# Attention's scores and values in 64x64 quarters of the PE array, and later places for splits, squares, a scaling and a row norm

## The chip, the cores and the metric

The kernel runs on one core of a Trainium2 chip. The metric is the device time of one execution, in microseconds (us). Engines are named as in the profile: PE (TensorE: matrix products and transposes), DVE (VectorE), ACT (ScalarE), POOL (GpSimd) and SP, which issues most DMAs. Each engine works through its own queue in order and they wait for one another by semaphores.

## What is computed

One layer of a streaming encoder over 320 tokens (256 of a new stream, 64 of a running one), width 2048, all in float32:

```python
z = rmsnorm(x, ln_g) @ w_in                       # 2048 -> q 1024, k 128, v 128, zs 2048
# group A: 16 query heads of 64 on 2 key/value heads, chunks of 64 tokens,
# each chunk sees itself and the 2 chunks before it (up to 192 keys)
s = einsum('...qhgd,...khd->...hgqk', q, k) * HEAD_DIM**-0.5 + bias
m = maximum(max(s, -1), sink); p = exp(s - m)
w = p / (sum(p, -1) + exp(sink - m))
attn_o = einsum('...hgqk,...khd->...qhgd', w, v)
# group B: gating, over chunks of 128 tokens
a = gelu(zs); u = a[..., :1024]; v = rmsnorm(a[..., 1024:], g)
sgu_o = u * (einsum('gij,bnjgc->bnigc', ws, v) + b_s)
# both groups
mix = concat([rmsnorm(attn_o, g_a), rmsnorm(sgu_o, g_s)])
x = x + mix @ w_out
h = rmsnorm(x, ln_ffn); y = x + square(relu(h @ w_up)) @ w_down      # 2048 -> 8192 -> 2048
```

Keys, values and the normalised gating rows of the running stream are outputs too.

## The kernel before

**Weights.** Everything is kept transposed: channels on the 128 partitions, the 320 tokens along the free axis. Each weight matrix is streamed from HBM in tiles of 512 x 256 (`w_raw`, 512 KB). A tile is split in two (`halves`): ACT writes the rounded part `w_hi` (L115), DVE the rest `w_lo` (L116), three buffers of each. The activations are split in the same way (`XH`/`XL`, `AH`/`AL`, `SH`/`SL`, ...). A product of a tile is then 24 PE instructions, three for each of 4 x 2 blocks of 128x128: high by high, high by low, low by high (L141). This document calls the work of one tile a step; `product` makes four steps for 256 output columns of `w_in`.

**Small work between the steps.** Attention and gating run during the projection by `w_in`. A function given in `between_pieces` under the number of a step is issued on PE right behind this step's last product, and the next step's products right behind the piece: `tc.issue_after` fixes this order, and `narrow` holds the last PE instruction of the piece. On the other engines the framework's planner sets the order of instructions, from the program's order, the dependencies and a simulated time line; `issue_after` only says what an instruction may not go ahead of on its engine.

**Attention** has ten units: 2 key/value heads (`kv`) x 5 chunks of queries. `attend(i)` is one piece and works on three units at once: it issues the scores of unit i, the transposes of unit i-2 and the values of unit i-3. Scores (L428) are products over the 64 channels of a head for two heads at a time, so they hold 64 rows by 128 columns of the PE array; `p` picks the upper or lower 64 rows, and each `p` writes its own PSUM bank `s_ps[p]` (one buffer each). Softmax runs on DVE (L438 to L448, L455, L456), ACT (L449, L453) and POOL (the division, L457). Transposes (L477) bring the probabilities into `misc` banks (two buffers), DVE copies them to `pts` (L500), and one `attend` later the values (L484, L489) multiply them by the values' rows: `va` for the first two 64-key parts, 128 rows by 64 columns, and `vb` for the third, 64x64. The result stands in columns 384 to 511 of the `misc` banks, and ACT copies it to `ao` (L495). Chunk 0 of a key/value head has 64 keys and only `vb`; chunk 1 has 128 keys and only `va`; chunks 2, 3 and 4 have 192 keys and both.

The pieces stand behind steps 1 and 3 of a product: `attend(0)` and `(1)` in q's last product, `attend(2)` to `(9)` in gating's four products for v, `attend(10)` to `(12)` in the first two products for u.

**Gating.** For v, `gelu2` gives `gv`; squares are summed on POOL into `acc_v` (`add_square`, L512), POOL scales `gv` and `gvs` by a gain (L539) and copies the last 64 sums (L540). `rows_norm` turns the sums into one factor per token: three small PE products (L166), DVE (L169) and a power on POOL (L171). `by_rows` transposes `gv` on PE (L551), and ACT writes it back with that factor (L553); its last call also issues two stores on POOL's queue. `spatial` (L564, L567) multiplies by the gating matrices.

**Behind attention**, in the loop over u's four products (L597), `split` makes `AH` (ACT, L205) and `AL` (DVE, L206) from `ao`, and `add_square` sums its squares into `acc_a`; `two_parts` and `rstd` turn that into the norm `rm_a`, a piece of the fourth product. `AH` and `AL` are first used by the product with `w_out`, and after it come the two large products with `w_up` and `w_down`.

Of the kernel before, what the change touches and what calls it, by code (L numbers as in the profile page):

```python
# [11 lines left out]
AF = mybir.ActivationFunctionType  # L12
# [3 lines left out]
P = 128  # L16
# [10 lines left out]
HD = 64  # L27
# [3 lines left out]
def hymba_step_kernel(ctx: ExitStack, tc: tile.TileContext, i, o):  # L31
# [378 lines left out]
    units = [(b, kv) for kv in range(2) for b in range(5)]  # L410
    probs = {}
    room = blk("vnat", [P, 2432])
# [5 lines left out]

    def scores(u):
        blk_, kv = units[u]  # L420
        q0, k0, nk, b0 = blocks[blk_][0:4]
        js = slice(2 * kv, 2 * kv + 2)
        s_ps = [score_bank(p) for p in range(2)]
        for j in range(2):
            a = 2 * (2 * kv + j)
            for p in range(2):
                hs = slice(p * HD, (p + 1) * HD)
                mm = nc.tensor.matmul(out=s_ps[p][:, j * nk:(j + 1) * nk],  # L428
                                      lhsT=qT[hs, blk_, a:a + 2].rearrange("p a t -> p (a t)"),
                                      rhs=kz[hs, kv, k0:k0 + nk], start=True, stop=True)  # L430
        last = mm
        s = at.tile([P, 2, 2, 192], F32, name="s", tag="s", bufs=2)
# [18 lines left out]
        for p in range(2):  # L451
            for j in range(2):
# [3 lines left out]
        nc.vector.reciprocal(out=den, in_=den)  # L456
        nc.gpsimd.tensor_tensor(out=sv, in0=sv,  # L457
                                in1=den[:, :, :, None].to_broadcast([P, 2, 2, nk]), op=ALU.mult)
        probs[u] = s
        return last  # L460

    def attend(i):

        t, v = i - 2, i - 3
        t, v = t if 0 <= t < 10 else None, v if 0 <= v < 10 else None
        if t is not None or v is not None:
            bank = [misc(), misc()] if t is not None else [score_bank(p) for p in range(2)]

# [4 lines left out]
        if t is not None:  # L473
            s = probs.pop(t).rearrange("x p j k -> x p (j k)")
            nk = blocks[units[t][0]][2]
            cols = ((P, 2),) if nk == HD else ((0, 0), (192, 1)) if nk == P else ((0, 0), (256, 1), (P, 2))
            behind([lambda p=p, x=x, c=c: nc.tensor.transpose(out=bank[p][:, x * P:(x + 1) * P], in_=s[:, p, c:c + P],  # L477
                                                              identity=ident) for p in range(2) for c, x in cols])
        if v is not None:
            blk_, kv = units[v]  # L480
            q0, va, vb = (blocks[blk_][x] for x in (0, 4, 5))
            out = lambda p, j: bank[j][p * HD:(p + 1) * HD, 384:512]
            if va is not None:
                behind([lambda p=p, j=j: nc.tensor.matmul(out=out(p, j), lhsT=va[j][:, kv],  # L484
                                                          rhs=pts[v % 2][p][:, j * P:(j + 1) * P], start=True,
                                                          stop=vb is None) for j in range(2) for p in range(2)])
            if vb is not None:
                hs = [slice(j * HD, (j + 1) * HD) for j in range(2)]
                behind([lambda p=p, j=j: nc.tensor.matmul(out=out(p, j), lhsT=vb[j][hs[j], kv], rhs=pts[v % 2][p][hs[j], 256:384],  # L489
                                                          start=va is None, stop=True) for p in range(2) for j in range(2)])  # L490
        if i < 10:
            behind([lambda: scores(i)])
        if v is not None:
            for j in range(2):
                nc.scalar.activation(out=ao[:, 4 * kv + 2 * j:4 * kv + 2 * j + 2, q0:q0 + 64],  # L495
                                     in_=bank[j][:, 384:512].rearrange("p (a q) -> p a q", a=2), func=AF.Copy)
        if t is not None:
# [33 lines left out]
    for g in range(4):  # L531
# [4 lines left out]
        for a in range(2 * g, 2 * g + 2):  # L536
            add_square(acc_v, gv[:, a], a == 0)
            for dst, c in ((gv[:, a, 0:256], slice(0, 256)), (gvs[:, a], slice(256, T))):
                nc.gpsimd.tensor_scalar(out=dst, in0=gv[:, a, c], scalar1=g_sv[:, a:a + 1], scalar2=None, op0=ALU.mult)  # L539
    nc.gpsimd.tensor_copy(out=acc_v[:, T:TP], in_=acc_v[:, 256:T])  # L540
# [36 lines left out]
    def rows_norm():  # L577
# [4 lines left out]
    u_pieces = {  # L582
        0: {1: lambda: attend(10), 3: lambda: (rows_norm(), attend(11))},
        1: {1: lambda: (attend(12), by_rows((0, 0), (1, 0))), 2: lambda: by_rows((0, 1), (1, 1), (2, 0)),
            3: lambda: spatial(0, 1, 2, 3)},
# [11 lines left out]
    for g in range(4):  # L597
        u_ps = product(w_in, 0, KT, 1280 + g * 256, xh, xl, between_pieces=u_pieces.get(g, {}))
        if g == 0:
            acc_a = sums("acc_a")  # L600
            AH, AL = blk("AH", [P, 8, T], F32R), blk("AL", [P, 8, T], F32R)
        for x in range(2):
            a, (high, low, _) = 2 * g + x, steps[2 * x + 1]
            with tc.issue_after(high), tc.issue_after(low):
                split(ao[:, a], g_oa[:, a:a + 1], AH[:, a], AL[:, a])
        for x, a in enumerate(range(3 * g, min(3 * g + 3, 8))):
            with tc.issue_after(steps[x][0]):
                add_square(acc_a, ao[:, a], a == 0)
# [131 lines left out]
```

## Time and profile before

| | |
|---|---|
| median of 3 runs | 1243.49 us (1242.76 to 1245.67) |
| the profiled execution's own time | 1243.31 us |
| its span, first to last instruction | 1241.5 us |
| PE busy | 1236.9 us, 8524 products and transposes |
| DVE busy | 658.6 us |
| ACT busy | 492.0 us |
| POOL busy | 108.3 us |
| granted PE clock | 1.00 of full speed |
| the products by `w_in` with all pieces (time line) | about 34.8 to 223.9 us |

PE's rows in the profile are modelled at their ends: instructions overlap in the array, and a row lasts longer than the distance to the next one. So the starts of successive rows are what is compared here. A float32 score or value product shows as two rows (two passes), a transpose as one.

### The profile page before, as it was taken

What the parts mean: (1) busy time and instruction counts of PE and PEld (TensorE: products, weight loads), DVE (VectorE), ACT (ScalarE), POOL (GpSimd) and SP (SyncE); (2) the same over time, 40 slices, a digit from 0 to 9 for tenths busy, and PEclk for the clock granted to TensorE, in tenths of its full rate; (3) what the DMA queues carried; (4) which work ended last, traced back from release to release, by engine and by line L of the source; (5) the groups of instructions that cost most, each with busy time, mean ns of one, the idle gap of its engine ahead of it and who ended that gap; (6) DMA issues with size and microseconds to landing.
All of it is one profiled execution on the core that took longest, in us unless ns stands there. A gap on an engine that the chain in (4) does not pass through costs nothing.

```text
span 1241.5 us, 20270 instructions
## 1 busy us (share of the span) xinstructions
PE 1236.9 (100%) x8524; PEld 1226.1 (99%) x8524; DVE 658.6 (53%) x781; ACT 492.0 (40%) x652; POOL 108.3 (9%) x109
## 2 busy tenths in 40 slices
PE   9999999999999999999999999999999999999998
PEld 8999999999999999999999999999999999999998
DVE  7877767977864443444444444444443344544343
ACT  7436555434533333223443233333333323433321
POOL 0137563201300000000000000000000000000000
PEclk9999999999999999999999999999999999999999
DMA  9753445444455444445544444545444444544550
GB/s 278 228 147 106 119 118 176 157 152 145 148 152 152 153 152 147 146 149 153 153 151 145 147 152 153 152 144 149 151 153 153 147 147 149 152 153 164 167 164 32
DMA packets 187995, 188.02 MB, mean 151 GB/s; under 512 B 7648, under 2 KB 187440, under 8 KB 187904
## 3 DMA queue, kind: packets, MB, share of 16 engines
q1 hardware_dynamic: 186640, 185.51, 48.0%
q0 software_dynamic: 832, 0.98, 0.4%
q8 instruction: 66, 1.08, 0.4%
q10 hardware_dynamic: 432, 0.24, 0.1%
q14 instruction: 25, 0.20, 0.0%
HBM read 183.13 MB, written 3.35 MB: 150 GB/s over the span
## 4 chain that ended last, share of the span: by engine, by line
PE 97%; POOL 1%; DMA 1%; DVE 0%; issue 0%; ACT 0%; SPq 0%; DVEq 0%; ACTq 0%; POOLq 0%
PE acc L141 92%; PE misc L141 1%; PE q_ps L237 1%; PE acc L237 1%; PE s_ps L428 1%; DMA w_first<-in_w_in 0%; PE misc L477 0%; DMA xT<-in_xT 0%; POOL acc_a L512 0%; PE misc L484 0%; PE misc L489 0%; PE misc L551 0%; PE g_ps L564 0%; PE misc L564 0%; ACT s L453 0%
## 5 line engine op out<-in xcount | busy, mean ns | idle before, releaser
L116 DVE TENSOR_TENSOR w_lo<-w_raw,w_hi 128x1024 fp32r<-128x1024 f32 x332 | 413.9, 1247 | 429.7 <-ACT w_hi L115 420.9
L115 ACT ACTIVATE w_hi<-w_raw 128x1024 fp32r<-128x1024 f32 x332 | 352.1, 1060 | 689.1 <-PE acc L141 662.7
L141 PE MATMUL acc<-H2H,w_lo 128*128 128x320 f32 x1024 | 316.4, 309 | 0.0
L141 PE MATMUL acc<-H2H,w_hi 128*128 128x320 f32 x1024 | 316.4, 309 | 0.0
L141 PE MATMUL acc<-H2L,w_hi 128*128 128x320 f32 x1024 | 316.4, 309 | 0.0
L141 PE MATMUL acc<-FH,w_hi 128*128 128x320 f32 x992 | 306.5, 309 | 0.0
L141 PE MATMUL acc<-FL,w_hi 128*128 128x320 f32 x992 | 306.5, 309 | 0.0
L141 PE MATMUL acc<-FH,w_lo 128*128 128x320 f32 x992 | 306.5, 309 | 0.0
L141 PEld LDWEIGHTS acc<-H2H,w_hi 128*128 128x128 f32 x1024 | 192.2, 188 | 0.0
L141 PEld LDWEIGHTS acc<-H2L,w_hi 128*128 128x128 f32 x1024 | 192.2, 188 | 0.0
L141 PEld LDWEIGHTS acc<-H2H,w_lo 128*128 128x128 f32 x1024 | 192.2, 188 | 0.0
L141 PEld LDWEIGHTS acc<-FH,w_hi 128*128 128x128 f32 x992 | 186.2, 188 | 0.0
L141 PEld LDWEIGHTS acc<-FL,w_hi 128*128 128x128 f32 x992 | 186.2, 188 | 0.0
L141 PEld LDWEIGHTS acc<-FH,w_lo 128*128 128x128 f32 x992 | 186.2, 188 | 0.0
L141 PE MATMUL acc<-XH,w_hi 128*128 128x320 f32 x352 | 110.7, 314 | 0.0
L141 PE MATMUL acc<-XH,w_lo 128*128 128x320 f32 x352 | 108.8, 309 | 0.0
L141 PE MATMUL acc<-XL,w_hi 128*128 128x320 f32 x352 | 108.7, 309 | 0.0
L141 PEld LDWEIGHTS acc<-XH,w_hi 128*128 128x128 f32 x352 | 66.1, 188 | 3.1 <-issue 2.5
L141 PEld LDWEIGHTS acc<-XL,w_hi 128*128 128x128 f32 x352 | 66.1, 188 | 0.0
L141 PEld LDWEIGHTS acc<-XH,w_lo 128*128 128x128 f32 x352 | 66.1, 188 | 0.0
L656 DVE SCALAR_TENSOR_TENSOR tf<-acc,r 128x640 f32<-128x640 f32 x32 | 26.4, 825 | 41.8 <-PE acc L141 41.8
L671 DVE TENSOR_TENSOR xT<-xT,acc 128x640 f32<-128x640 f32 x31 | 25.5, 821 | 41.8 <-PE acc L141 41.8
(227 smaller groups left out, 1062.9 us busy)
## 6 DMA issues: line engine op xcount, KB each, us to landing
w_raw<-in_w_up SPq DMA_DIRECT2D x128, 512.0 KB
w_raw<-in_w_down SPq DMA_DIRECT2D x128, 512.0 KB
w_raw<-in_w_in SPq DMA_DIRECT2D x44, 512.0 KB
w_raw<-in_w_out SPq DMA_DIRECT2D x32, 512.0 KB
w_first<-in_w_in SPq DMA_DIRECT2D x14, 256.0 KB
out_yT<-xT SPq DMA_DIRECT2D x7, 320.0 KB
xT<-in_xT SPq DMA_DIRECT2D x8, 160.0 KB
xT<-in_xT SPq DMA_DIRECT2D x4, 320.0 KB
```

The source lines that it names most:

```text
L115: return (pin(nc.scalar.activation(out=hi, in_=raw, func=AF.Copy)).ins, pin(nc.vector.tensor_tensor(out=lo, in0=raw, in1=hi.bitcast(F32), ...
L116: pin(nc.vector.tensor_tensor(out=lo, in0=raw, in1=hi.bitcast(F32), op=ALU.subtract)).ins)
L141: mm = nc.tensor.matmul(out=out, lhsT=w_[:, k, g * P:(g + 1) * P], rhs=r_(kk), start=(kk == 0 and x == 0), stop=(kk == nk - 1 and x == 2))
L237: mm = nc.tensor.matmul(out=ps[:, 0:T], lhsT=w_[:, j, k, g * P:(g + 1) * P], rhs=r_(a + k), start=(a + k == 0 and x == 0), stop=(a + k == ...
L428: mm = nc.tensor.matmul(out=s_ps[p][:, j * nk:(j + 1) * nk], lhsT=qT[hs, blk_, a:a + 2].rearrange("p a t -> p (a t)"), rhs=kz[hs, kv, k0:k ...
L656: nc.vector.scalar_tensor_tensor(out=t, in0=ps[:, :, 0:T], scalar=0.0, in1=r2[:, None, :].to_broadcast([P, 2, T]), op0=ALU.max, op1=ALU.mult)
L671: nc.vector.tensor_tensor(out=xT[:, a, c], in0=xT[:, a, c], in1=p, op=ALU.add)
```

## The change

1. **Scores.** Each product of 64x128 becomes two of 64x64: the two heads of a pair go to the left and the right half of the array (`x`), the upper or lower rows as before (`p`). Scores are issued before the values of the same piece, no longer behind them; the softmax is its own function, issued behind the values.
2. **Values.** The products of 128 rows by 64 columns become two of 64x64, each over 64 of the 128 keys. The two halves `r` of a sum are written to different banks, the half with `r == j` together with the third part; `side` says where: columns 384 to 511 of the `misc` and `s_ps` banks (in `attend(12)` columns 0 to 127 of `s_ps` too). ACT copies one of them to `ao`, and DVE adds the other (a new instruction for each `j` of a unit with `va`, 16 in all).
3. **Gating's last scaling** (the four POOL instructions L539 of the fourth product for v) is put behind the last unit's division on POOL.
4. **The rows' norm** moves from behind step 3 of u's first product to behind step 1 of its second, ahead of `attend(12)`; one of the transposes by rows, `(1, 0)`, moves from there to behind step 2.
5. **Splits and squares of `ao`.** Splits of the 8 blocks were 2, 2, 2, 2 over u's four products and are 0, 3, 3, 2; squares were 3, 3, 2, 0 and are 0, 4, 4, 0.

```diff
-    def scores(u):
+    def scores(u, s_ps):
+        blk_, kv = units[u]
+        q0, k0, nk, b0 = blocks[blk_][0:4]
+        for j in range(2):
+            a = 2 * (2 * kv + j)
+            for x, p in [(x, p) for x in range(2) for p in range(2)]:
+                hs = slice(p * HD, (p + 1) * HD)
+                mm = nc.tensor.matmul(out=s_ps[p][x * HD:(x + 1) * HD, j * nk:(j + 1) * nk], lhsT=qT[hs, blk_, a + x],
+                                      rhs=kz[hs, kv, k0:k0 + nk], start=True, stop=True)
+        return mm
+
+    def softmax(u, s_ps):
         blk_, kv = units[u]
         q0, k0, nk, b0 = blocks[blk_][0:4]
         js = slice(2 * kv, 2 * kv + 2)
-        s_ps = [score_bank(p) for p in range(2)]
-        for j in range(2):
-            a = 2 * (2 * kv + j)
-            for p in range(2):
-                hs = slice(p * HD, (p + 1) * HD)
-                mm = nc.tensor.matmul(out=s_ps[p][:, j * nk:(j + 1) * nk],
-                                      lhsT=qT[hs, blk_, a:a + 2].rearrange("p a t -> p (a t)"),
-                                      rhs=kz[hs, kv, k0:k0 + nk], start=True, stop=True)
-        last = mm
         s = at.tile([P, 2, 2, 192], F32, name="s", tag="s", bufs=2)
...
-        nc.gpsimd.tensor_tensor(out=sv, in0=sv,
-                                in1=den[:, :, :, None].to_broadcast([P, 2, 2, nk]), op=ALU.mult)
+        ready[:] = [nc.gpsimd.tensor_tensor(out=sv, in0=sv, in1=den[:, :, :, None].to_broadcast([P, 2, 2, nk]),
+                                            op=ALU.mult).ins]
         probs[u] = s
-        return last
...
-        if t is not None or v is not None:
-            bank = [misc(), misc()] if t is not None else [score_bank(p) for p in range(2)]
+        bank = [misc(), misc()] if t is not None else None
+        s_ps = [score_bank(p) for p in range(2)]
...
+        if i < 10:
+            behind([lambda: scores(i, s_ps)])
         if v is not None:
             blk_, kv = units[v]
             q0, va, vb = (blocks[blk_][x] for x in (0, 4, 5))
-            out = lambda p, j: bank[j][p * HD:(p + 1) * HD, 384:512]
-            if va is not None:
-                behind([lambda p=p, j=j: nc.tensor.matmul(out=out(p, j), lhsT=va[j][:, kv],
-                                                          rhs=pts[v % 2][p][:, j * P:(j + 1) * P], start=True,
-                                                          stop=vb is None) for j in range(2) for p in range(2)])
-            if vb is not None:
-                hs = [slice(j * HD, (j + 1) * HD) for j in range(2)]
-                behind([lambda p=p, j=j: nc.tensor.matmul(out=out(p, j), lhsT=vb[j][hs[j], kv], rhs=pts[v % 2][p][hs[j], 256:384],
-                                                          start=va is None, stop=True) for p in range(2) for j in range(2)])
+            hs = [slice(r * HD, (r + 1) * HD) for r in range(2)]
+            side = {(r, j): bank[r][:, 384:512] if bank and j == 0 else s_ps[r][:, 384:512] if j else s_ps[r][:, 0:P]
+                    for r in range(2) for j in range(2)}
+
+            def part(r, j, p, span):
+                lhsT, c = (va[j][hs[r], kv], slice(j * P, (j + 1) * P)) if span < 2 else (vb[j][hs[j], kv], slice(256, 384))
+                return nc.tensor.matmul(out=side[r, j][hs[p]], lhsT=lhsT, rhs=pts[v % 2][p][hs[r], c],
+                                        start=span < 2 or va is None, stop=span == 2 or vb is None or r != j)
+
+            turns = [x for x in (0, 2, 1) if (va, va, vb)[x] is not None]
+            behind([lambda r=r, p=p, x=x: part(r, 1 - r if x == 1 else r, p, x) for x in turns for r in range(2) for p in range(2)])
         if i < 10:
-            behind([lambda: scores(i)])
+            softmax(i, s_ps)
         if v is not None:
             for j in range(2):
-                nc.scalar.activation(out=ao[:, 4 * kv + 2 * j:4 * kv + 2 * j + 2, q0:q0 + 64],
-                                     in_=bank[j][:, 384:512].rearrange("p (a q) -> p a q", a=2), func=AF.Copy)
+                dst = ao[:, 4 * kv + 2 * j:4 * kv + 2 * j + 2, q0:q0 + 64]
+                nc.scalar.activation(out=dst, in_=side[j, j].rearrange("p (a q) -> p a q", a=2), func=AF.Copy)
+                if va is not None:
+                    nc.vector.tensor_tensor(out=dst, in0=dst, in1=side[1 - j, j].rearrange("p (a q) -> p a q", a=2), op=ALU.add)
...
             for dst, c in ((gv[:, a, 0:256], slice(0, 256)), (gvs[:, a], slice(256, T))):
-                nc.gpsimd.tensor_scalar(out=dst, in0=gv[:, a, c], scalar1=g_sv[:, a:a + 1], scalar2=None, op0=ALU.mult)
+                with tc.issue_after(ready[0]) if g == 3 else nullcontext():
+                    nc.gpsimd.tensor_scalar(out=dst, in0=gv[:, a, c], scalar1=g_sv[:, a:a + 1], scalar2=None, op0=ALU.mult)
...
-        0: {1: lambda: attend(10), 3: lambda: (rows_norm(), attend(11))},
-        1: {1: lambda: (attend(12), by_rows((0, 0), (1, 0))), 2: lambda: by_rows((0, 1), (1, 1), (2, 0)),
+        0: {1: lambda: attend(10), 3: lambda: attend(11)},
+        1: {1: lambda: (rows_norm(), attend(12), by_rows((0, 0))), 2: lambda: by_rows((1, 0), (0, 1), (1, 1), (2, 0)),
             3: lambda: spatial(0, 1, 2, 3)},
...
-        for x in range(2):
-            a, (high, low, _) = 2 * g + x, steps[2 * x + 1]
+        for x, a in enumerate(((), (0, 1, 2), (3, 4, 5), (6, 7))[g]):
+            high, low, _ = steps[x + 1]
             with tc.issue_after(high), tc.issue_after(low):
                 split(ao[:, a], g_oa[:, a:a + 1], AH[:, a], AL[:, a])
-        for x, a in enumerate(range(3 * g, min(3 * g + 3, 8))):
+        for x, a in enumerate(((), (0, 1, 2, 3), (4, 5, 6, 7), ())[g]):
             with tc.issue_after(steps[x][0]):
                 add_square(acc_a, ao[:, a], a == 0)
```

More of the change, by code (lines that the diff above doesn't have):

```diff
@@ L410, in hymba_step_kernel @@
     units = [(b, kv) for kv in range(2) for b in range(5)]
-    probs = {}
+    probs, ready = {}, []
     room = blk("vnat", [P, 2432])
```

## The prediction

> **What bounds the kernel now.** I read the page first, then PE's waits, then PE's time line around one `attend`.
>
> ```profile
> span 1241.5 us, 20270 instructions
> ...
> PE 1236.9 (100%) x8524; PEld 1226.1 (99%) x8524; DVE 658.6 (53%) x781; ACT 492.0 (40%) x652; POOL 108.3 (9%) x109
> ```
>
> ```profile
> PE misc L166 <- POOL acc_v L540: 0.4, 1, 0.4
> PE q_ps L237 <- ACT w_hi L115: 0.4, 1, 0.4
> ```
>
> PE works through the whole span. In the pieces it waits for another engine in one place only, L166. So an edit is worth what it takes from PE's queue, or from that wait; on another engine it counts only if PE comes to wait for it. A busy PE says nothing of how tightly its rows follow each other, so here is `attend(5)` (transposes, `va`, `vb`, scores of 64 keys, next step):
>
> ```profile
> 115.17 0.82 PE L477 MATMUL misc<-ident,s 128*128 128x128 f32 x6
> 115.92 0.32 PE L484 MATMUL misc<-kzv 128*64 128x128 f32 x1
> 115.93 0.32 PE L484 MATMUL misc<-vnat,kzv 128*64 128x128 f32 x1
> 116.08 0.27 PE L484 MATMUL misc<-kzv 128*64 128x128 f32 x1
> 116.09 0.27 PE L484 MATMUL misc<-vnat,kzv 128*64 128x128 f32 x1
> 116.19 0.27 PE L484 MATMUL misc<-kzv 128*64 128x128 f32 x1
> 116.20 0.27 PE L484 MATMUL misc<-vnat,kzv 128*64 128x128 f32 x1
> 116.30 0.27 PE L484 MATMUL misc<-kzv 128*64 128x128 f32 x1
> 116.31 0.27 PE L484 MATMUL misc<-vnat,kzv 128*64 128x128 f32 x1
> 116.51 0.33 PE L489 MATMUL misc<-kzv 64*64 64x128 f32 x2
> 116.52 0.33 PE L489 MATMUL misc<-vnat,kzv 64*64 64x128 f32 x2
> 116.67 0.28 PE L489 MATMUL misc<-kzv 64*64 64x128 f32 x2
> 116.68 0.28 PE L489 MATMUL misc<-vnat,kzv 64*64 64x128 f32 x2
> 116.89 0.66 PE L428 MATMUL s_ps<-kzv,qT 64*128 64x64 f32 x8
> 117.48 0.41 PE L141 MATMUL acc<-XH,w_hi 128*128 128x320 f32 x1
> ```
>
> Rows that use different parts of the array start 0.01 apart, so they run together; call such a set a beat. `va` is four beats of two, `vb` two beats of four (two quarters of each half of the rows). The starts of `va` are 0.16, 0.11 and 0.11 apart, and 0.21 lie between its last beat and the first of `vb`. The next shape again begins with 0.16 and ends with 0.21. So a beat costs 0.11, and **each change of the array's division costs 0.15 more**: 0.10 before the new shape starts, 0.05 because its first weights (64 columns) load with nothing to hide behind.
>
> The scores have four beats too. This is the chain, with start and length, for 192 and 128 keys:
>
> ```profile
> 88.16 0.85 PE s_ps L428 x8
> ...
> 126.41 0.65 PE s_ps L428 x8
> ```
>
> 128 keys: 4 x 0.11 + 0.10 leave 0.11 for the first load, which is 128 columns wide. 192 keys: 4 x 0.16 + 0.10 + 0.11 = 0.85. 64 keys take 117.48 - 116.89 = 0.59, only 0.06 less than 128: the beat stays near 0.11, the time of a 128-column load.
>
> **The change part by part.**
>
> *Scores and values.* Beats: scores keep 4 per unit (two `j`, two passes; each now has four quarters in place of two halves), 40 in all. Values keep 2 for chunk 0, 4 for chunk 1, 6 for the others, 24 per key/value head, 48 in all. So no beat goes; changes of division do. Scores, `va` and `vb` had a division each, and all are 64x64 now. That takes away one change in `attend(3)`, `(4)`, `(8)`, `(9)` (one kind of values), two in `(5)`, `(6)`, `(7)`, and one in `(10)` to `(12)` (no scores): 4 + 6 + 3 = 13 x 0.15 = 1.95 us. The first load of the ten score groups is 64 columns wide: 10 x (0.11 - 0.05) = 0.6 us. The 64-key beats of two units lose the wide load that held them at 0.11; they end between 0.11 (no gain) and 0.06 (half the elements of a 0.11 beat). I take 0.06, since a 64-column load showed 0.05: 2 x 3 x 0.05 = 0.3 us. Sum 2.85; the last of four quarters starts 0.01 to 0.02 later than the last of two, 0.1 us over the pieces: **2.75 us**.
>
> What before does not show is a third beat of four quarters. Lower bound: 0.11, as in `va`, where the loads of the following beat are hidden. Upper bounds: 0.16 if each beat waits for its load as the second of `vb` did, or 0.22 if four quarters run as two pairs. I take 0.11: in `va`, too, the second beat stood at 0.16 and the third at 0.11, and the four of `vb` did start together.
>
> *The rows' norm.* PE's time line where it stands now, and the instructions behind its waits:
>
> ```profile
> 170.48 0.50 PE L166 MATMUL misc<-inv_1k,acc_v 128*128 128x1 f32 x4
> 171.37 0.38 PE L166 MATMUL misc<-inv_1k,acc_v 128*128 128x1 f32 x2 [0.39 <-POOL acc_v L540]
> 171.61 1.01 PE L477 MATMUL misc<-ident,s 128*128 128x128 f32 x6
> 172.55 0.32 PE L484 MATMUL misc<-kzv 128*64 128x128 f32 x1
> ```
>
> ```profile
> 170.81 0.50 POOL L540 COPY acc_v<-acc_v 128x64 f32<-128x64 f32 x1
> ...
> 172.11 1.86 POOL L171 TENSOR_TENSOR rs_rows<-r_rows,nhalf 128x3 f32<-128x3 f32 x1
> ```
>
> ```profile
> 171.87 0.14 DVE L169 TENSOR_SCALAR r_rows<-misc 128x3 f32<-128x3 f32 x1
> ```
>
> L166 lasts 171.61 - 170.48 = 1.13 us; six beats of 0.11 would be 0.66, so it waits 0.47. The transposes behind it take 0.94 against 0.75 in `attend(5)`: the second half needs the bank that L169 reads until 172.01, 0.19 us. L540 came less than 1 us too late (171.31). The new place is two whole steps later, so L540 is long done there, and `attend(12)` takes no `misc` bank: **0.66 us**. The six products themselves move and cost the same. L169 and L171 move too; ACT's first row copy waits for L171, which ended 172.11 + 1.86, 2.5 us behind L166, so ACT stands still for up to that time. The two stores by POOL's queue stay behind the same step, and no transfer on SP's queue moves.
>
> *Work off PE.* DVE gets 16 additions. The nearest row is an addition out of PSUM of the same size:
>
> ```profile
> L573 DVE TENSOR_TENSOR gv<-misc,sgb x2: 274/278/281, 193.9 to 202.3; 128x128 f32<-128x128 f32 x2
> ```
>
> 16 x 0.28 = 4.5 us, 0.56 per `attend`. Five of them fall into the stretch of this row (PE, PEld, DVE, ACT, POOL):
>
> ```profile
> 97.50:154.50 57.00, 57.00 (x456) 52.93 (x455) 45.33 (x96) 34.10 (x96) 36.47 (x33) 1.00 0.41 116
> ```
>
> DVE has 57.00 - 45.33 = 11.7 us free there and gets 2.8. Each addition waits for ACT's copy to the same columns, and behind it on DVE stand `pts` and the next `w_lo`. The shortest lead of `w_lo` over its products among the 20 steps from 98 to 187 us is this pair, 140.16 - 134.68 = 5.5 us:
>
> ```profile
> 132.96 1.72 DVE L116 TENSOR_TENSOR w_lo<-w_raw,w_hi 128x1024 fp32r<-128x1024 f32 x1 [0.58 <-ACT w_hi L115]
> ```
>
> ```profile
> 140.16 0.31 PE L141 MATMUL acc<-XH,w_lo 128*128 128x320 f32 x1
> ```
>
> I cost the additions at nothing. Without that lead they would cost their 4.5 us. The splits and squares leave u's first product and stand in its second to fourth. The four squares of the third, with their additions on POOL, must be done before the first of these products, the last splits before the second, which stand two and four steps behind the third product's end:
>
> ```profile
> 216.57 0.31 PE L186 MATMUL misc<-n_hl,mean_1k 128*128 128x320 f32 x1
> ...
> 223.90 0.31 PE L141 MATMUL acc<-AH,w_hi 128*128 128x320 f32 x1
> ```
>
> Gating's last scaling then waits on POOL for the last softmax; its readers are transposes behind step 2 of u's second product, three steps behind the norm's old place. Both at nothing.
>
> *Sum.* 2.75 + 0.66 = 3.4 us from the profiled execution's 1243.31 (its span and 1.8 around it), of which PE's stream is the whole middle: 1239.9. The median lies 0.18 above that execution: **1240.0 us**.
>
> **The rivals.**
>
> *Loads in the open.* Each beat of quarters waits for its own weights: 0.16. Of 88 beats, 13 open a group and have that already; 75 x 0.05 = 3.75 us more: 1243.8. For it: the only second beat of quarters seen stands at 0.16. Against: so does the second of `va`. The Trainium skill, "TensorE: Matmul & The Clock Gate", Part 3 (row/col tiling), says that a weight load overlaps running products only where the row group differs; two quarters always share one, so by that rule this rival holds. The trace disagrees for 128x64, where all rows are shared and the beat is 0.11; for a row of quarters no run here shows it yet.
>
> *Pairs, the slower side.* Four quarters in one beat are possible for the two passes of `vb`, but a longer row of them is taken two by two. Scores: 6 x 4 x 0.16 + 2 x 4 x 0.11 + 2 x 4 x 0.06 = 5.2; values 48 x 0.11 = 5.3; 10.5 more: 1250.5. It decides from a beat 3.4 / 75 = 0.045 above 0.11. Against it: the four starts within 0.02 in `vb`.
>
> *A new wait on PE.* The `s_ps` banks now also hold sums, so scores wait for ACT's copies and DVE's additions of the `attend` before, not only for L438. In `attend(9)` the room is
>
> ```profile
> 157.42 0.73 DVE L438 SCALAR_TENSOR_TENSOR s<-s_ps,rq,bias 128x192 f32<-128x192 f32 x2
> ```
>
> ```profile
> 161.62 0.38 PE L477 MATMUL misc<-ident,s 128*128 128x128 f32 x2
> ```
>
> from 158.15 to 161.62, 3.5 us, into which a copy, an addition and a `w_lo` of 1.2 fit. Or `spatial` waits for row copies that L171 made late. I price it at 1 to 3 us in all: 1241 to 1243. The Trainium skill, "TensorEngine Tiling (Array Packing)", PSUM Bottleneck, warns of this side: emptying PSUM may become the bound once the array is tiled. DVE's 11.7 us free speak against it here.
>
> *The division is not what costs 0.15.* If a new source or bank costs it, the changes stay and only L166's 0.66 is gained: 1242.8.
>
> **How the numbers follow.** Forecast 0.66, open loads 0.12, new wait 0.12, pairs 0.05, division 0.05. A median of this kernel is told from no change at about 0.2%, 2.5 us: faster is below 1241.0. Runs lie some 1 us apart, so the forecast gives 0.58 faster and 0.08 same; new waits 0.02 faster, 0.09 same, 0.01 slower; open loads 0.11 same, 0.01 slower; division 0.05 same; pairs slower. Faster 0.60, same 0.33, slower 0.07. Low end: the forecast less 1.4 (the runs' own spread, and beats below 0.06). High end: 1244.0, which takes in open loads and leaves out pairs.
>
> **What would show it.** `attend(5)` from its first row behind the transposes to the next step (117.48 - 115.92 = 1.56 us) should shrink to about 1.05, with sets of four starts within 0.02 and sets 0.11 apart; 0.16 or 0.22 apart names the rival. L166 should show no wait, and PE's waits no new line. Scores (`s_ps`) or L564 waiting for DVE or ACT, or `w_lo` ending behind its step's start, would make the forecast wrong.

## The result and the profile after

The median went from 1243.95 us (1242.76 to 1245.67) to 1241.02 us (1240.14 to 1241.86), measured side by side. The ratio is 0.9978, with a 95% interval of 0.9969 to 0.9987. So the kernel is 2.9 us faster, where 1240.0 us and 3.5 us had been forecast from the first median. The profiled execution took 1240.81 us.

The page of the kernel after (span 1239.0 us), engines:

```profile
PE 1234.3 (100%) x8668; PEld 1225.1 (99%) x8668; DVE 664.0 (54%) x797; ACT 492.1 (40%) x652; POOL 106.4 (9%) x109
```

PE has 144 instructions more and is busy 2.6 us less. Its waits for other engines in the pieces are now this one:

```profile
PE misc L478 <- DVE vnat L507: 0.3, 1, 0.3
```

The wait at L166 is gone, and the line is new: the transposes (L478, formerly L477) wait for DVE's copy of probabilities (L507, formerly L500). The stretch that answers to the prediction's `attend(5)`, from the time line of the kernel after (start, length, instruction); scores now stand ahead of the values:

```profile
115.67 0.46 PE L426 MATMUL s_ps<-kzv,qT 64*64 64x64 f32 x16
115.95 0.27 PE L491 MATMUL misc<-kzv 64*64 64x128 f32 x1
115.95 0.27 PE L491 MATMUL s_ps<-kzv 64*64 64x128 f32 x1
115.96 0.27 PE L491 MATMUL misc<-vnat,kzv 64*64 64x128 f32 x1
115.97 0.27 PE L491 MATMUL s_ps<-vnat,kzv 64*64 64x128 f32 x1
116.06 0.27 PE L491 MATMUL misc<-kzv 64*64 64x128 f32 x1
...
116.50 0.27 PE L491 MATMUL s_ps<-kzv 64*64 64x128 f32 x1
...
116.72 0.41 PE L141 MATMUL acc<-XH,w_hi 128*128 128x320 f32 x1
```

Four quarters start within 0.02, and the sets stand 0.11 apart, the second as the last: the six first starts go from 115.95 to 116.50, 5 x 0.11. From the first row behind the transposes to the next step there are 116.72 - 115.67 = 1.05 us, where before had 1.56. All four 64-key beats of scores, first load and all, fit into 0.28 us.

The part that did not come as forecast is `attend(11)`. PE's time line of the kernel after:

```profile
168.51 0.49 PE L478 MATMUL misc<-ident,s 128*128 128x128 f32 x3
169.34 0.52 PE L478 MATMUL misc<-ident,s 128*128 128x128 f32 x3 [0.34 <-DVE vnat L507]
169.79 0.32 PE L491 MATMUL misc<-kzv 64*64 64x128 f32 x1
```

The six transposes take 169.79 - 168.51 = 1.28 us, 0.53 more than the 0.75 of `attend(5)` before. Their second half needs the second `misc` bank, which DVE empties late. DVE and POOL of the kernel after show why, in two time lines:

```profile
165.44 2.43 DVE L116 TENSOR_TENSOR w_lo<-w_raw,w_hi 128x1024 fp32r<-128x1024 f32 x1 [0.29 <-ACT w_hi L115]
167.79 0.54 DVE L507 COPY kzv<-misc 128x384 f32<-128x384 f32 x1
168.26 0.27 DVE L503 TENSOR_TENSOR ao<-ao,s_ps 128x128 f32<-128x128 f32 x1
168.45 0.27 DVE L503 TENSOR_TENSOR ao<-ao,misc 128x128 f32<-128x128 f32 x1
168.65 0.54 DVE L507 COPY vnat<-misc 128x384 f32<-128x384 f32 x1
```

```profile
164.98 0.23 POOL L548 COPY acc_v<-acc_v 128x64 f32<-128x64 f32 x1
165.32 1.47 POOL L459 TENSOR_TENSOR s<-s,den 128x768 f32<-128x768 f32 x1
166.77 1.89 POOL L547 TENSOR_SCALAR gv<-gv,cols 128x256 f32<-128x256 f32 x1
...
169.06 0.92 POOL L547 TENSOR_SCALAR gv<-gv,cols 128x256 f32<-128x256 f32 x1
```

A `w_lo` of 2.43 us, twice its usual 1.22, stands ahead of the first copy, and two of the new additions (0.2 us each until the next start) ahead of the second. The copy ends at 168.65 + 0.54 = 169.19, and the transposes go on 0.15 us later. The table by stretch (PE, PEld, DVE, ACT, POOL busy, with counts; then clock, DMA share, GB/s), before and then after:

```profile
155.00:182.00 27.00, 26.61 (x212) 24.79 (x211) 18.62 (x32) 14.50 (x31) 17.83 (x15) 1.00 0.38 107
```

```profile
97.50:154.50 57.00, 57.00 (x565) 54.45 (x564) 45.67 (x102) 32.59 (x91) 36.73 (x33) 1.00 0.39 109
155.00:182.00 27.00, 26.66 (x240) 25.49 (x239) 23.76 (x42) 15.77 (x36) 16.85 (x14) 1.00 0.48 132
```

In the stretch that the prediction looked at, DVE stands where it stood (45.33 and 45.67). From 155 to 182 us, where the new wait lies, it went from 18.62 to 23.76 us of 27. A full DVE does not make the wait by itself: in a later run (halves exchanged, additions left out) it is busy 23.97 us of the same 27, and PE waits for nothing there.

Piece by piece, PE's time between the last product ahead of a piece and the first behind it gives this account (us saved; "forecast" are the prediction's own terms put where they belong, before its 0.1 for later starts):

| | forecast | measured |
|---|---|---|
| `attend(0)` to `(4)` | 0.21, 0.06, 0.06, 0.21, 0.21 | 0.20, 0.05, 0.04, 0.20, 0.19 |
| `attend(5)` to `(9)` | 0.51, 0.36, 0.36, 0.21, 0.21 | 0.51, 0.36, 0.35, 0.20, 0.19 |
| `attend(10)` | 0.15 | 0.12 |
| `attend(11)`, `(12)` and the norm | 0.96 | 0.53 |
| sum | 3.51 | 2.93 |

In the two profiled executions the first score instruction starts at 72.16 us (before) and 72.58 us (after). No changed instruction stands ahead of it on PE. Waits at the kernel's start, which differ from one execution to the next, had cost the one of after 0.42 us by then, so its span is shorter by 2.5 and not by 2.9.

### The profile page after: what moved, and what is told of

Its sections match the earlier page's. It is cut to its first block, busy times and chain, and to the rows that moved or that the text cites. A ratio compares the mean times of both kernels' runs of the same rounds, so it can differ in the third digit from the quotient of the medians.

```text
span 1239.0 us, 20602 instructions
## 1 busy us (share of the span) xinstructions
PE 1234.3 (100%) x8668; PEld 1225.1 (99%) x8668; DVE 664.0 (54%) x797; ACT 492.1 (40%) x652; POOL 106.4 (9%) x109
## 4 chain that ended last, share of the span: by engine, by line
PE 95%; DMA 3%; SPq 1%; DVE 1%; ACT 0%; issue 0%; DVEq 0%; ACTq 0%
PE acc L141 92%; PE misc L141 1%; DMA w_raw<-in_w_in 1%; SPq L110 1%; DMA w_first<-in_w_in 1%; DMA xT<-in_xT 1%; PE s_ps L426 1%; PE misc L478 0%; PE misc L491 0%; ACT w_hi L115 0%; DVE w_lo L116 0%; PE s_ps L491 0%; PE g_ps L572 0%; PE misc L572 0%; PE misc L559 0%
```

## The experiments

### Each half of the change alone, and scores alone

Quarters with everything else left where it was (parts 1 and 2 of the change):

```diff
-                with tc.issue_after(ready[0]) if g == 3 else nullcontext():
...
-        0: {1: lambda: attend(10), 3: lambda: attend(11)},
+        0: {1: lambda: attend(10), 3: lambda: (rows_norm(), attend(11))},
...
+            a, (high, low, _) = 2 * g + x, steps[2 * x + 1]
...
+        for x, a in enumerate(range(3 * g, min(3 * g + 3, 8))):
```

> Parts 1 and 2 of the change alone (scores and values in quarters, the additions); the scaling, the rows' norm, splits and squares stand as before. Theory (the parts add up): attend(0) to attend(12) lose 2.7 us of PE's queue, with the same lengths as in the changed kernel, and L166 keeps a wait of about 0.5 us: 2.7 us faster than the kernel before. Rival (L166 is a fixed date): POOL's copy L540 ends as late as before (171.3 us), because POOL's own chain sets it, and PE only comes earlier to it: attend(0) to (10) lose 2.4 us, L166 waits up to 2.4 us longer (0.5 to 2.9), and the whole is 0.3 us faster. Between the two the wait of L166 tells how much of the gain was lost there.

Measured: 1246.7 us against 1243.62, ratio 1.0027 (1.0017 to 1.0037). The quarters alone make the kernel slower by 3 us, which neither expectation had, though `attend(0)` to `(9)` save on PE exactly what they save in the whole change. `attend(10)` takes 0.34 us more and not 0.15 less, with a wait of 0.3 for DVE's copy (L507). The rest is lost at the norm. PE's time line there, and POOL's copy of the last sums:

```profile
169.38 0.60 PE L166 MATMUL misc<-inv_1k,acc_v 128*128 128x1 f32 x4 [0.54 <-POOL acc_v L519]
173.04 0.59 PE L166 MATMUL misc<-inv_1k,acc_v 128*128 128x1 f32 x2 [3.06 <-POOL acc_v L547]
173.49 1.52 PE L478 MATMUL misc<-ident,s 128*128 128x128 f32 x6
174.94 0.47 PE L491 MATMUL misc<-kzv 64*64 64x128 f32 x1
```

```profile
172.49 0.49 POOL L547 COPY acc_v<-acc_v 128x64 f32<-128x64 f32 x1
```

The wait of 0.47 us has become one of 3.6 (0.54 and 3.06). PE's first row of the norm stands 1.1 us sooner than before (169.38, not 170.48), although it has waited already, and POOL's copy of the last sums ends 1.7 us later (172.98, not 171.31). While PE stands, its clock falls. The table by stretch of the same kernel, PE alone (busy, granted clock):

```profile
169.00:173.00 4.00, 0.60 (x4) 0.72 0.44 130
173.00:174.90 1.90, 1.86 (x8) 0.50 0.85 258
174.90:176.40 1.50, 1.50 (x25) 0.50 0.23 51
176.40:184.20 7.80, 7.80 (x56) 0.93 0.20 64
```

The mean of 0.72 from 169 to 173 us is full speed until about 170.75 and half from there on; by the mean of 0.93 in the last row, half speed ends at about 177.5. At 0.50 the six transposes take 174.94 - 173.49 = 1.45 us and not 0.75, and the quarters' beats stand 0.21 apart and not 0.11. The Trainium skill, "TensorE: Matmul & The Clock Gate", Part 1, gives the clock two settings, full and half, and lets it fall after an idle window of about 3.4 us. The trace agrees on the settings (1.00 and 0.50), but not on so long an idle time: the clock fell 1.9 us behind the end of PE's last product (168.84 us), with four rows of the norm in between.

The other half alone (parts 3, 4 and 5; scores and values as before), and, as a third kernel, scores alone in quarters:

```diff
+                with tc.issue_after(ready[0]) if g == 3 else nullcontext():
...
+        1: {1: lambda: (rows_norm(), attend(12), by_rows((0, 0))), 2: lambda: by_rows((1, 0), (0, 1), (1, 1), (2, 0)),
...
+            high, low, _ = steps[x + 1]
```

> Parts 3, 4 and 5 alone: the scaling behind the last division, the rows' norm behind step 1 of u's second product, splits and squares later; scores and values as before. Theory (the parts add up): the attends keep their lengths, L166's six rows take 0.66 us in their new place with no wait, the transposes of attend(11) take 0.75 us again: 0.66 us faster than before, in the trace, which is within what repeated runs can tell from no change. Rival (the moves are what made a new wait in attend(11), because the scaling now runs on POOL beside DVE's w_lo): the transposes of attend(11) wait about 0.5 us as in the changed kernel, and only about 0.2 us is gained.

```diff
-            for p in range(2):
+            for x, p in [(x, p) for x in range(2) for p in range(2)]:
                 hs = slice(p * HD, (p + 1) * HD)
-                mm = nc.tensor.matmul(out=s_ps[p][:, j * nk:(j + 1) * nk],
-                                      lhsT=qT[hs, blk_, a:a + 2].rearrange("p a t -> p (a t)"),
+                mm = nc.tensor.matmul(out=s_ps[p][x * HD:(x + 1) * HD, j * nk:(j + 1) * nk], lhsT=qT[hs, blk_, a + x],
```

> The kernel before, with the scores alone in quarters; they stay behind the values, and the values stay 128x64 (va) and 64x64 (vb), so no additions. Theory (a change of division costs 0.15 us): the change from vb to scores goes in attend(3), (5), (6), (7), (8), the first load of ten score groups is 0.05 shorter, and the 64-key beats shrink from 0.11 to 0.06: 5 x 0.15 + 10 x 0.05 + 6 x 0.05 = 1.55 us less in the attends; attend(5) 0.36, attend(6) and (7) 0.20, attend(4) and (9) 0.05. Rival (another source or bank costs the 0.15, not the division): the change from vb to scores stays as dear, 0.8 us less in the attends, attend(6) and (7) 0.05. If L166 waits for a fixed date, its wait grows by what the attends lost.

The moves alone: 1242.91 us against 1243.62, ratio 0.9994 (0.9985 to 1.0003), which the runs cannot tell from no change. On PE the norm's pieces save 0.76 us, 0.1 more than the 0.66 of the forecast: in their new place the six products add 0.57 to the pieces. Scores alone: 1242.41 us, ratio 0.9989 (0.9980 to 0.9998); the pieces save 1.54 us, where 0.15 for each change of the division, 0.05 for each first load and 0.15 for each 64-key unit had given 1.55. So the price of a change of the division holds; the values then still stand in 128x64 and the wait at L166 is as before (0.4).

The two halves measure +3.1 and -0.7 us (the second within the noise); together they give -2.9. The parts don't add: beside the quarters the moves are worth about 6 us, and not 0.66, because they take away a wait that the quarters make.

### What eats DVE's lead: the additions?

`w_lo` had led its products by at least 5.5 us; in the kernel after the smallest lead is at the step whose first `w_lo` product starts at 156.25 + 2 x 0.15 = 156.54, behind this row:

```profile
153.11 2.15 DVE L116 TENSOR_TENSOR w_lo<-w_raw,w_hi 128x1024 fp32r<-128x1024 f32 x1 [0.57 <-ACT w_hi L115]
```

This is 156.54 - 155.26 = 1.3 us. The first suspect was the 16 additions. In the next kernel they are left out, and with them one half of each sum:

```diff
-                if va is not None:
-                    nc.vector.tensor_tensor(out=dst, in0=dst, in1=side[1 - j, j].rearrange("p (a q) -> p a q", a=2), op=ALU.add)
```

> The changed kernel without DVE's 16 additions: the second half of each sum of values is left out of the output. Theory (the additions eat the lead of w_lo and make the wait of attend(11)): the shortest lead of w_lo between 100 and 185 us rises from 1.3 to over 4 us, and the transposes of attend(11) take 0.75 instead of 1.28 us. Rival (POOL's scaling, moved beside a w_lo that took 2.43 instead of 1.22 us, makes it): that w_lo stays above 2 us, the transposes of attend(11) stay above 1.0 us and the shortest lead below 3 us.

The profiled execution took 1240.73 us. The smallest lead is 0.31 us, shorter still, and PE's new wait moved from `attend(11)` to `attend(10)` (0.5 us, for the same kind of copy of `pt`). At `attend(11)` the transposes take 0.74 us again, though the `w_lo` ahead of the copies still takes 2.43: there the two additions did make the copy late, but without them another comes late elsewhere. The theory that the additions eat the lead falls. ACT's waits named another suspect. They had a new first line in the kernel after (ACT's waits from 95 to 190 us):

```profile
ACT ao L501 <- DVE s L440: 12.9, 7, 2.7
```

By this line ACT's copy out of an `s_ps` bank stands behind DVE's reading of the scores in the same bank, 12.9 us in all, and behind ACT's copy stand its next `w_hi` and its exponentials.

### ACT copies from `misc`, DVE adds from `s_ps`

One line exchanges the halves of the sums, so that ACT copies out of the `misc` banks again and DVE adds out of `s_ps`, which it reads for the scores anyway:

```diff
-            side = {(r, j): bank[r][:, 384:512] if bank and j == 0 else s_ps[r][:, 384:512] if j else s_ps[r][:, 0:P]
+            side = {(r, j): bank[r][:, 384:512] if bank and r == j else s_ps[r][:, 384:512] if bank or r == j else s_ps[r][:, 0:P]
```

> The changed kernel with the halves of the sums swapped between the banks: the one that ACT copies always stands in a misc bank, the one that DVE adds in s_ps; the instructions are the same. Theory (ACT stands at its copy out of s_ps until DVE has read the scores from that bank, 12.9 us in all, and that is what made w_hi, w_lo and the copies to pts late): that wait falls below 1 us, the shortest lead of w_lo between 100 and 185 us returns from 1.3 to 4 us or more, the transposes of attend(11) take 0.75 instead of 1.28 us, and the time is about 0.5 us below the changed kernel, 1240.5. Rival (DVE is simply fuller by 16 additions, or the planner's order is worse): leads stay below 3 us and attend(11) keeps its wait.

Measured: 1239.99 us (1239.48 to 1240.8) against 1243.98, ratio 0.9968 (0.9956 to 0.9980). ACT's wait for L440 is gone. From 60 to 200 us PE has no wait left, and at `attend(11)` its time line reads

```profile
168.10 0.82 PE L478 MATMUL misc<-ident,s 128*128 128x128 f32 x6
168.84 0.32 PE L491 MATMUL misc<-kzv 64*64 64x128 f32 x1
```

The transposes take 0.74 again. `attend(11)`, `(12)` and the norm save 1.06 us and not 0.53, `attend(10)` its full 0.15, and all pieces together 3.49 us beside the forecast's 3.51. So the 0.5 us came from the banks that ACT and DVE were given to read. The smallest lead rose to 2.3 us only; what takes the rest of the 5.5 is not settled. Summing both halves in one bank, with no addition at all, was not tried. The interval of this ratio overlaps with that of the change itself, so that this version is the faster by some 0.5 us rests on PE's pieces, not on the medians.

The same without the additions (again half of each sum left out):

> The run copies_from_misc without DVE's 16 additions: the second half of each sum of values is left out of the output. It closes the square of the two causes of the lost lead of w_lo (5.5 us before; 1.3 with ACT's copy out of s_ps and additions, 0.3 without additions, 2.3 with the copies out of misc and additions). Theory (both eat of it, one hidden behind the other): with neither, the shortest lead between 95 and 188 us is 4 us or more. Rival (the additions eat nothing; what is left of the loss comes from the order of scores, values and softmax): it stays at 2 to 3 us.

The profiled execution took 1241.95 us, but its first score instruction starts 2.0 us later than in the kernel with the additions, at the start of the kernel; from there on every piece has the same time within 0.01 us. The smallest lead is 1.8 us, below what either expectation had. With ACT out of the way, the 16 additions cost PE nothing.

### Which of the moves carries the change

Quarters alone again, with the halves exchanged as above:

> Parts 1 and 2 alone, as in the run quarters_only, with the same swap of banks. Theory (two lates met there: POOL's chain was 1.7 us later than before because of ACT's standing at s_ps, and PE 2.4 us earlier): L540 ends between 169.4 (it moves with PE) and 171.3 us (it does not) instead of 173.0, L166 waits 1 to 3 us instead of 3.6, PE's clock falls for a shorter time or not at all, and the whole comes to 1241.5 to 1244. Rival (the bank has no part in it): L540 ends near 173.0 again and the time is 1246.7.

Measured: 1246.0 us, ratio 1.0018 (1.0008 to 1.0027), nearly as slow and 2 us above the expected range. POOL's copy now ends at 170.17 and PE waits only 1.1 us at L166. But the transposes behind it, the next in line for the norm's bank, wait for DVE (PE's time line, then DVE's):

```profile
170.74 0.53 PE L478 MATMUL misc<-ident,s 128*128 128x128 f32 x3
173.40 0.66 PE L478 MATMUL misc<-ident,s 128*128 128x128 f32 x3 [2.13 <-DVE r_rows L169]
```

```profile
170.51 1.56 DVE L116 TENSOR_TENSOR w_lo<-w_raw,w_hi 128x1024 fp32r<-128x1024 f32 x1
172.00 0.54 DVE L206 SCALAR_TENSOR_TENSOR AL<-ao,cols,AH 128x320 fp32r<-128x320 f32 x1
172.46 0.81 DVE L524 TENSOR_TENSOR z<-acc,rx 128x640 f32<-128x640 f32 x1
173.20 0.15 DVE L169 TENSOR_SCALAR r_rows<-misc 128x3 f32<-128x3 f32 x1
```

L169 needs 0.15 us and stands behind a `w_lo`, a split and an eviction, 2.7 us of work (170.51 to 173.20). The wait of 0.19 us in the prediction has grown to 2.1, and the clock stands at 0.50 from 174 to 177 us. Next, quarters with the norm moved (parts 1, 2 and 4):

> Parts 1, 2 and 4: the quarters and the rows' norm in its later place; the scaling, splits and squares as before. Theory (the norm's date was the whole loss of quarters_only): no wait on PE above 0.5 us, within 0.5 us of the changed kernel, 1241. Rival (the division of the last unit is late on POOL too, behind the scaling and acc_a: it ended at 170.7 in quarters_only, and PE comes to the transposes of attend(11) at 168.5): these transposes wait about 2 us for POOL, and only about 1 us of the gain is left, 1242.5 to 1243.5.

1243.21 us, ratio 0.9993 (0.9984 to 1.0002): 3.5 us less than quarters alone, as L166 waits no longer, but `attend(11)` does:

```profile
170.44 0.88 PE L478 MATMUL misc<-ident,s 128*128 128x128 f32 x6 [1.97 <-POOL s L459]
```

```profile
166.36 1.79 POOL L519 TENSOR_TENSOR acc_a<-acc_a,sq 128x320 f32<-128x320 f32 x1
168.11 0.86 POOL L519 TENSOR_TENSOR acc_v<-acc_v,sq 128x320 f32<-128x320 f32 x1
168.93 1.46 POOL L459 TENSOR_TENSOR s<-s,den 128x768 f32<-128x768 f32 x1
```

The last unit's division is behind a row of POOL's work, squares of `ao` and gating's scaling (until 166.39) among it. Two kernels ask which of these it is. They start from the version with the halves exchanged and put back the splits and squares (part 5) or the scaling (part 3):

```diff
-        for x, a in enumerate(((), (0, 1, 2), (3, 4, 5), (6, 7))[g]):
-            high, low, _ = steps[x + 1]
+        for x in range(2):
+            a, (high, low, _) = 2 * g + x, steps[2 * x + 1]
...
-        for x, a in enumerate(((), (0, 1, 2, 3), (4, 5, 6, 7), ())[g]):
+        for x, a in enumerate(range(3 * g, min(3 * g + 3, 8))):
```

> The run copies_from_misc with part 5 undone: splits and squares 2, 2, 2, 2 and 3, 3, 2, 0 again. Theory (part 3 is what frees the last division on POOL): no wait on PE above 0.2 us, the time that of copies_from_misc, 1240. Rival (the additions to acc_a, 1.8 us each on POOL, keep it late by themselves): the transposes of attend(11) wait 0.5 to 1.5 us.

```diff
-                with tc.issue_after(ready[0]) if g == 3 else nullcontext():
-                    nc.gpsimd.tensor_scalar(out=dst, in0=gv[:, a, c], scalar1=g_sv[:, a:a + 1], scalar2=None, op0=ALU.mult)
+                nc.gpsimd.tensor_scalar(out=dst, in0=gv[:, a, c], scalar1=g_sv[:, a:a + 1], scalar2=None, op0=ALU.mult)
```

> The run copies_from_misc with part 3 undone: gating's last scaling where the planner puts it, no longer behind the last division. Theory (with ACT's standing gone, POOL has room: the scaling takes 4.2 us from about 160.5, the division then ends at about 167.5, PE comes at 168.1): no wait above 0.3 us. Rival (part 3 is needed in any case): the transposes of attend(11) wait 1 us or more for POOL's division.

Of both there is the profiled execution only, so PE's pieces decide. With the splits and squares early (1244.29 us) `attend(11)` takes 2.86 us more, with a new wait, and the two steps behind it another 0.95, at a granted clock of 0.50 from 172 to 175 us. PE's row, then DVE's `w_lo` and the two copies behind it:

```profile
170.53 1.18 PE L478 MATMUL misc<-ident,s 128*128 128x128 f32 x6 [1.75 <-POOL gv L547]
```

```profile
167.22 2.49 DVE L116 TENSOR_TENSOR w_lo<-w_raw,w_hi 128x1024 fp32r<-128x1024 f32 x1 [0.94 <-ACT w_hi L115]
...
169.84 0.55 DVE L507 COPY kzv<-misc 128x384 f32<-128x384 f32 x1
...
170.50 0.55 DVE L507 COPY vnat<-misc 128x384 f32<-128x384 f32 x1
```

The profile names POOL, whose scaling ended at 170.51. But the transposes read nothing of it, and the bank that they write came free at 169.84 + 0.55 = 170.39, one weight load (0.14 us) ahead of their start. The second half of the transposes starts at 171.19, the same 0.14 behind the end of the second copy (170.50 + 0.55 = 171.05). I read it as DVE's copies again, late behind the same doubled `w_lo`; the trace speaks for them, and no run separates the two. With the scaling early (1240.67 us) every piece takes the same as without (within 0.01 us); its first score instruction starts 0.82 us later, more than the 0.74 by which the profiled execution is longer. So the late splits and squares are needed, and the late scaling is worth nothing once they have left POOL. The norm's later place is needed where the other moves are missing. Beside them it may not be: in the whole change POOL's copy of the last sums ends at 164.98 + 0.23 = 165.21 us (L548, shown above) and PE comes to `attend(11)` at 168.51, so L166 would have nothing to wait for in its old place. Whether the transposes would then wait behind L169 no run shows.

### The price of a division, from the other side

Scores issued ahead of the transposes, not behind them, in the version with the halves exchanged: in the seven pieces that have transposes and values the array goes from 128x128 to quarters, back, and to quarters again, two changes more in each:

```diff
+        if i < 10:
+            behind([lambda: scores(i, s_ps)])
         if t is not None:
...
-        if i < 10:
-            behind([lambda: scores(i, s_ps)])
         if v is not None:
```

> The run copies_from_misc with the scores ahead of the transposes, so that in attend(3) to (9) the 128x128 transposes stand between two groups of 64x64 products; same instructions. Theory (each change of the array's division costs 0.15 us): two more changes in seven pieces, 14 x 0.15 = 2.1 us, 0.30 in each of attend(3) to (9), none in attend(2): 1242.1 us. Rival (a change costs only where it also changes source or bank, or the gain of the quarters came from something else): attend(3) to (9) stay within 0.1 us and the time is 1240.

Measured: 1242.37 us against 1243.8, ratio 0.9989 (0.9979 to 0.9998); beside the version it starts from, seven pieces lose 0.31 us each, 2.15 in all, for 14 changes: 0.154 us for one. The price read off the trace of before (0.15) is right in both directions.

## Why the prediction was right, and where it was not

**The price of the division, 0.15 us: right.** Thirteen fewer changes, and fourteen more, both give it; with the halves exchanged no new wait is mixed in. The rival that a new source or bank costs the 0.15 is refuted by the last experiment, where a piece has as many changes of source and bank as before and only the division changes more often.

**First loads and 64-key beats: right.** `attend(1)` and `(2)` have nothing but the first load and save 0.05 and 0.04 (0.06 forecast). `attend(0)` adds a 64-key unit and saves 0.20 (0.21).

**The third beat of quarters at 0.11: right.** The choice between bounds fell on the lower one, by the row of `va`. The rivals *loads in the open* (0.16) and *pairs* (0.22) would both show in the rows of `attend(5)` above; every beat behind the second stands at 0.11. By the rule of the Trainium skill, "TensorE: Matmul & The Clock Gate", Part 3, that a load overlaps only where the row group differs, they would have stood at 0.16: the trace disagrees for quarters as it did for 128x64.

**The norm's 0.66: right for the move alone** (0.76 measured), but not as a term of this sum. It was costed in the schedule of before, where POOL was less than 1 us late. Beside the quarters the same wait is 3.6 us and brings the lower clock with it. The whole change never meets that wait, and the prediction gave the norm's place alone the credit: POOL's copy ends 6 us earlier there (165.21, not 171.31), which the other moves may do without it. For the change without parts 3 to 5 the same method gave -2.7 us, and +3.1 was measured. That the whole came near the forecast is in this part luck.

**Work off PE at nothing: the step that was mis-sized.** It cost 0.5 us at `attend(11)`, nearly all of what the change fell short by. The rival *a new wait on PE* had the right kind of place, the banks that hold sums, but the wrong victim (scores, `spatial`) and too high a price (1 to 3 us). Exchanging one pair of halves takes this cost away, which shows that it came from the banks. The chain between is read from the traces: ACT's copies out of `s_ps` wait for DVE's scores; softmax and `w_hi` behind them come later; DVE's work bunches up; the copies out of `misc` come late; the transposes wait. The doubled `w_lo` is not enough by itself: in the moves alone one takes 2.42 us in the same place, and PE waits for nothing. The prediction asked of DVE whether 4.5 us fit into its room and whether `w_lo` would be in time. It did not ask who is made to wait at a bank that now has readers on two engines, and it read DVE's room from 97 to 154 us, not from 155 to 182, where the wait arose. Free room was the wrong thing to read in either place: what counts is when a copy comes.

**Splits, squares and scaling at nothing: right for the last, half right for the others.** Nothing waits for them where they stand now; but where they stood they would have cost nearly 4 us beside the quarters. An edit costed at nothing was one that the gain depended on.

## What to carry to other kernels

Count the changes of the array's division in a piece and order the work so that they are few; here each cost 0.15 us, and quarters of 64x64 ran four abreast with their loads hidden. When PE gets faster, ask at once which engine it now catches up with: a wait of half a microsecond can become one of 3.6, and the lower clock behind a stall can cost nearly as much again. Let one engine empty a PSUM bank, or at least don't put the copy of a second engine behind the slow readers of the first.

## What was not expected of the hardware

**A stall is paid twice.** In quarters alone PE waited 3.6 us, and the granted clock was 0.50 from about 170.75 to 177.5 us; PE was at work for 4.5 us of this, so that the clock cost some 2.3 us more (an estimate: half of 4.5). With the splits early PE stood for 1.9 us (counted from when its next row was due) and, between the halves of the transposes, 0.3 more. The clock fell at about 171.8, when PE had gone on already, and stayed at 0.50 until 175.2. The remaining 1.6 of the 3.8 us are left for the clock.

**DVE and POOL take turns.** In the rows of the kernel after, `w_lo` starts at 165.44, 0.12 behind POOL's L459 (1.47 us), and takes 2.43 us: the rest of L459, 1.35, and 1.08 from there on, near the 1.22 that it takes alone. L547, the next on POOL, takes 1.89 us and not 0.92: `w_lo` ends 1.10 us after L547's start. With the scaling early the same `w_lo` got there first, and POOL's division took the longer time (DVE's and POOL's time lines of that kernel):

```profile
165.04 1.22 DVE L116 TENSOR_TENSOR w_lo<-w_raw,w_hi 128x1024 fp32r<-128x1024 f32 x1
```

```profile
165.28 2.31 POOL L459 TENSOR_TENSOR s<-s,den 128x768 f32<-128x768 f32 x1 [0.41 <-DVE den L458]
```

Here L459 is longer by 2.31 - 1.47 = 0.84 us, about the 0.98 that `w_lo` still had to run. The Trainium skill, "SBUF — State Buffer", section "SBUF: two separate sides", describes this as an exclusive lock, held for the whole instruction by whichever started first, for a DVE instruction with two inputs in SBUF; these rows agree. A busy POOL thus takes DVE's time too: the same `w_lo` costs DVE 2.43 us or 1.22, by which of the two comes first. A sum made with the time that a row takes alone leaves this out.
